# Hi and lo halves of normed inputs side by side: one 512-column matmul in place of two 256-column ones

## Chip, cores and metric

The kernel runs on one core of one Trainium2 chip. The metric is the device time of one execution in microseconds (us), less is better. The time before is 1701.62 us, the median of three runs (1701.26 to 1703.69).

## The reference, cut to what matters

One sequence of 256 tokens, 1024 wide, goes through a first block (a mixer, a cross-attention on a memory, a mixture of 32 experts) and then through two layers of a second block. All arithmetic is in float32. The change touches products of a normed input with a weight matrix: the queries of the cross-attention, and in each layer of the second block the hyena and the query/key projections and the first product of the feed-forward part.

```python
x = x + memory_cross_attention(rms_norm(x, g_xattn), rms_norm(mem, g_mem), w_q_x, w_kv_x, w_o_x)
...
for i in range(2):                                   # second block
    h = _rms_norm(x, norm_mix_pre[i])
    proj = h @ w_in[i]
    u_hy, q, k, v, g_out, gate_lr, u_pool, gate_logits = _split(proj, IN_SPLITS)
    y_hy = _hyena_mixer(u_hy, ...)                   # starts with a convolution over 3 tokens
    y_gla = _gla_mixer(q, k, v, g_out, gate_lr, ...) # q is scaled by 128 ** -0.5
    ...
    h = _rms_norm(x, norm_ffn_pre[i])
    a, b = _split(h @ ffn_w_up[i], (2816, 2816))
    a = _dwconv3_centred(a, ffn_conv_w[i], ffn_conv_b[i])
    y = (jax.nn.gelu(a, approximate=False) * b) @ ffn_w_down[i]
    x = x + _rms_norm(y, norm_ffn_post[i])
```

## The kernel before, in words

TensorE takes operands in a shortened float32 format (F32R). To keep float32 accuracy each operand is kept as two parts, hi (the rounded value) and lo (what the rounding left), and a product is made of three matmuls: hi times hi, hi times lo and lo times hi. `mm3` (lines 329 to 338) issues the three. Where the weights are the stationary operand they stand at lines 336 (weights' hi, input's hi), 337 (weights' hi, input's lo) and 338 (weights' lo, input's hi); where the input is stationary they stand at 332 to 334.

`norm` (line 430) makes a normed input: two tiles `hh` and `hl` of 128 partitions x 8 x 256 (feature within a group of 128, group, token), filled by transposes. `dense_t` (line 367) multiplies such an input with a "chunk" of weights, 1024 x 128 numbers held as 128 x 1024, and leaves the result transposed (128 output features x 256 tokens). A call handles two chunks, both into one bank of PSUM (the accumulators `acc`, four banks of 128 x 512), each in 8 steps over the features, so 8 x 3 matmuls of 256 columns for a chunk. These steps are called k-steps here. Then `consume(ps)` takes the bank off:
- for `w_q_x` (line 740) and `w_qk0`, `w_qk1` (line 1489) with one ScalarE copy of 128 x 512;
- for `w_hy0`, `w_hy1` (`hconv`, line 1496) with `conv3` (line 1328) twice, which reads PSUM with one ScalarE and two VectorE instructions (lines 1331, 1332, 1333);
- for `w_up0`, `w_up1` (`glu`, line 1648) with `conv3` on the one half, a Gelu on ScalarE (1651), a multiply by the other half on VectorE (1652) and a split of the result into hi and lo (455 on ScalarE, 456 on VectorE).

The weights come from HBM as plain float32 (`raw`) through the SP queue and are split on the chip, for each chunk: ScalarE writes `whi` (line 455, 128 x 1024), VectorE `wlo` (line 456). There are 5 buffers for `whi` (`NH`), 4 for `wlo` (`NL`). A split waits until the buffer is free, that is until TensorE has read the chunk that was in it.

The inputs that come out of `norm` with the pool `self.norms` are those of `w_q_x` (8 chunks), `w_qk` (8 chunks a layer), `w_hy` (12 chunks a layer) and `w_up` (40 chunks a layer): 128 chunks, 1024 k-steps, 3072 matmuls. Other inputs (`g_mix`, `g_mem`) use the same function with another pool. The same inputs also enter `dense_n`, where they are stationary and the weights stream in 512 columns (gates, values, pool).

The order of instructions on each engine is fixed when the program is built: a planner lists them by readiness and program order. On the chip each engine takes its own queue in that order, so an instruction that waits holds up what is queued behind it on its engine.

Of the kernel before, what the change touches and what calls it, by code (L numbers as in the profile page):

```python
# [22 lines left out]
F32 = mybir.dt.float32  # L23
F32R = mybir.dt.float32r
I32 = mybir.dt.int32
BF16 = mybir.dt.bfloat16
AF = mybir.ActivationFunctionType
OP = mybir.AluOpType
# [3 lines left out]
P = 128  # L32
D = 1024
S = 256
# [216 lines left out]
class Kernel:  # L251
# [114 lines left out]

    def dense_t(self, xT, name, chunks, consume):

        hi, lo = xT
        ps = self.acc().rearrange("p (j s) -> p j s", s=S)  # L370
        for j, chunk in enumerate(chunks):
            wh, wl = self.weights(name, chunk)
            for k in range(8):
                c = slice(k * P, k * P + P)
                self.mm3(ps[:, j], hi[:, k], lo[:, k], wh[:, c], wl[:, c], False, k == 0, k == 7)
        consume(ps)

# [50 lines left out]
    def norm(self, gname, pool, tag, g=None):  # L430

        nc = self.nc
        hi = pool.tile([P, 8, S], F32R, name=tag + "h", tag=tag + "h")
        lo = pool.tile([P, 8, S], F32R, name=tag + "l", tag=tag + "l")
        g = g or self.bcast(gname)

        def fill(t, xt, xg=None, r=None):
            if xg is None:
                xg, r = scaled(xt)
            nc.vector.tensor_scalar(xg[:, :512], xg[:, :512], r, None, op0=OP.mult)  # L440
            nc.scalar.activation(xg[:, 512:], xg[:, 512:], AF.Copy, scale=r)
            self.to_T(xg, hi, lo, t)

        def scaled(xt):
            ss = self.squares((xt[:, :512], xt[:, 512:]))
            xg = self.junk.tile([P, D], F32, name="xn", bufs=2)
            self.gained(xt, g, xg, 0)
            r = self.inv_norm(ss)
            self.gained(xt, g, xg, 1)
            return xg, r  # L450
        return (hi, lo), fill

    def split(self, hi, lo, src):

# [43 lines left out]
    def block1(self, outer, moe):  # L498
        nc, tc = self.nc, self.tc
        mm = nc.tensor.matmul  # L500
        x = self.x
        with ExitStack() as ctx:
            mix = ctx.enter_context(ExitStack())
            a = mix.enter_context(tc.tile_pool(name="mix", bufs=1, reuse_waits="tile"))

            nc.sync.dma_start(x[:, 0], self.ins["x"][0])
            hT, fill = self.norm("g_mix", outer, "hT")
# [63 lines left out]
            for t in range(2):  # L571
                ps = self.tp()
# [164 lines left out]
            self.load()  # L737
            qT = outer.tile([P, 8, S], F32, name="qk")
            for c in range(4):
                self.dense_t(qT_in, "w_q_x", (2 * c, 2 * c + 1), lambda ps, c=c: nc.scalar.activation(qT[:, 2 * c:2 * c + 2], ps, AF.Copy))  # L740
                if c < EARLY - 1:
                    self.load()
            sx = 1.0 / 16.0
# [38 lines left out]
            nc.sync.dma_start(wr, self.ins["w_r"])  # L782
            wr = wr.rearrange("p (k n) -> p k n", n=36)
            br = self.bcast("b_r", 0, 36, a, "br")
            hh, hl = (self.norms.tile([P, 2, D], F32R, name="h" + n, tag="h" + n) for n in "hl")
            L, W = (self.const.tile([P, 2, n], F32, name=k) for k, n in (("L", 36), ("W", NE)))
            A = self.const.tile([P, 2, NE], BF16, name="A")

# [569 lines left out]
    def mix(self, l, hT):  # L1358
# [3 lines left out]
        with ExitStack() as ctx:  # L1362
# [79 lines left out]
            nc.vector.tensor_sub(wlr[:, :, 96:], raw[:, :, 96:], wlr[:, :, 96:].bitcast(F32))  # L1442
            ps = self.acc()[:, :S]
            for k in range(8):
                for h in hT:
                    mm(ps, wlr[:, k], h[:, k], start=k == 0 and h is hT[0], stop=k == 7 and h is hT[1])
            lr = a.tile([P, S], F32R, name="lr")
            nc.scalar.activation(lr, ps, AF.Copy)
# [37 lines left out]

            qk = a.tile([P, 8, S], F32, name="qk", tag="qk")
            for c in range(4):
                self.dense_t(hT, f"w_qk{l}", (2 * c, 2 * c + 1), lambda ps, c=c: nc.scalar.activation(
                    qk[:, 2 * c:2 * c + 2], ps, AF.Copy, scale=P ** -0.5 if c < 2 else 1.0))  # L1490

            hw, hb = load(f"hy_conv_w{l}", [12, 3]), load(f"hy_conv_b{l}", [12])
            xv = a.tile([P, 8, S], F32, name="xv")
# [1 line left out]

            def hconv(n):
                def f(ps):
                    for j in range(2):
                        m = n + j
                        self.conv3(xv[:, m - 4] if m >= 4 else x0[:, m], ps[:, j], hw[:, m], hb[:, m:m + 1])  # L1500
                return f
            for n in (4, 8, 6, 10):
                self.dense_t(hT, f"w_hy{l}", (n, n + 1), hconv(n))
# [132 lines left out]
    def ffn(self, l, hT):  # L1636
        nc, tc = self.nc, self.tc
        x = self.x
        with ExitStack() as ctx:
            a = ctx.enter_context(tc.tile_pool(name=f"ffn{l}", bufs=1, reuse_waits="tile"))  # L1640
            cw = a.tile([P, NF, 3], F32, name="cw")
            nc.sync.dma_start(cw.rearrange("p a b -> p (a b)"), self.ins[f"ffn_conv_w{l}"])
            cb = a.tile([P, NF], F32, name="cb")
            nc.sync.dma_start(cb, self.ins[f"ffn_conv_b{l}"])
            hi, lo = (a.tile([P, NF, S], F32R, name="act" + n) for n in "hl")
            LEAD = 8

            def glu(j, ps):
                y = a.tile([P, S], F32, name="y", bufs=3)
                self.conv3(y, ps[:, 0], cw[:, j], cb[:, j:j + 1])  # L1650
                nc.scalar.activation(y, y, AF.Gelu)
                nc.vector.tensor_mul(y, ps[:, 1], y)
                self.split(hi[:, j], lo[:, j], y)
            for j in range(2):
                ps = self.tp()
                for n in range(4):
                    i, t = divmod(n, 2)
                    nc.tensor.transpose(ps[:, n * P:(n + 1) * P], self.up[:, t, (2 * j + i) * P:(2 * j + i + 1) * P], self.ident)
                glu(j, ps.rearrange("p (i s) -> p i s", i=2))
            for j in range(2, NF):  # L1660
                self.dense_t(hT, f"w_up{l}", (2 * j - 4, 2 * j - 3), partial(glu, j))
            g = self.bcast(f"norm_ffn_post{l}")
            ps = [[self.acc() for n in range(2)] for t in range(2)]
            if l == 0:
                hT, fill = self.norm("norm_mix_pre1", self.norms, "h")
            last = NF - LEAD
            ws = {}
            order = [(k, t, n) for k in range(last) for t in range(2) for n in range(2)]
            for k, t, n in order + ([(k, t, n) for t in range(2) for k in range(last, NF) for n in range(2)] if l == 0 else [(k, t, n) for t in range(2) for n in range(2) for k in range(last, NF)]):
                if k not in ws:  # L1670
                    ws[k] = self.weights(f"w_down{l}", k, k in range(last, NF - 4) and self.room(a, (f"held{k}",)))
                wh, wl = ws[k]
                tok, c = slice(t * P, (t + 1) * P), slice(n * 512, (n + 1) * 512)
                self.mm3(ps[t][n], hi[:, k, tok], lo[:, k, tok], wh[:, c], wl[:, c], True, k == 0, k == NF - 1)
                if k == NF - 1:
                    with tc.high_priority(100):
                        if n == 0:
                            take, end = self.post(g, t)
                        take(n, ps[t][n])
                        if n:  # L1680
                            end(None if l == 0 else lambda n, xn: nc.sync.dma_start(self.out[t][:, n * 512:(n + 1) * 512], xn))
                            if l == 0:
                                fill(t, x[:, t])
            return hT
# [21 lines left out]
```

## Time and profile before

| | us |
|---|---|
| median of three runs | 1701.62 |
| the profiled execution, timed | 1706.44 |
| its span in the profile | 1704.6 |
| TensorE matmul busy (share of the span) | 1635.3 (96%) |
| TensorE weight load busy | 1380.2 (81%) |
| VectorE busy | 1288.6 (76%) |
| ScalarE busy | 1133.9 (67%) |

PE is TensorE, PEld its weight loads, DVE VectorE, ACT ScalarE. A matmul's record runs from its start to the end of its result, and the records of neighbours overlap: its duration is not what it costs in a stream, which is the distance from its start to the start of the next. The mixture of experts lies between about 260 and 800 us; the second block from about 810 us to the end. In it the products with a transposed result lie at 878 to 935 us (`w_qk0`, `w_hy0`), 1078 to 1192 (`w_up0`), 1321 to 1378 (`w_qk1`, `w_hy1`) and 1522 to 1637 (`w_up1`); those of `w_q_x` at 170 to 194.

### The profile page before, as it was taken

The numbers are of one execution on the slowest core, as the hardware profiler recorded it, in microseconds if no ns is written. First come the engines' busy times: TensorE is split into PE (matmuls) and PEld (weight loads), VectorE is DVE, ScalarE is ACT, GpSimd is POOL, SyncE is SP. The second block draws the span as 40 slices with busy tenths as digits, with TensorE's granted clock in tenths as the row PEclk, the third lists the DMA queues.
The fourth block names the chain that finished last, engine by engine and source line by source line (L and its number), as shares of the span: only waits on it lengthen the run. The fifth ranks groups of instructions, "written<-read, shape, count | busy, mean of one in ns | idle before, by whom it ended". The sixth has DMA issues, their size and how long they took to land. (4 is left out here: it accounts for less than half of the span.)

```text
span 1704.6 us, 24749 instructions
## 1 busy us (share of the span) xinstructions
PE 1635.3 (96%) x9115; PEld 1380.2 (81%) x9115; DVE 1288.6 (76%) x1702; ACT 1133.9 (67%) x1576; POOL 30.3 (2%) x47
## 2 busy tenths in 40 slices
PE   7999987999999999988999999999999999999998
PEld 6897875777767777766799887999878998789986
DVE  7876566999989999998569667677556886667763
ACT  7765437899878899986667545555445864555552
POOL 1000000000000000000000000000000000000000
PEclk9999998999999999999999999999999999999999
DMA  8546537999999999994775356455756545635561
GB/s 292 199 155 204 191 148 266 352 380 373 381 380 380 402 386 408 416 400 170 253 252 186 128 189 223 143 185 182 238 171 222 202 150 181 214 130 185 183 198 62
DMA packets 94448, 415.92 MB, mean 244 GB/s; under 512 B 12324, under 2 KB 18868, under 8 KB 68468
## 3 DMA queue, kind: packets, MB, share of 16 engines
q1 hardware_dynamic: 89220, 405.91, 65.6%
q0 software_dynamic: 864, 6.29, 1.0%
q10 hardware_dynamic: 4240, 2.10, 0.4%
q8 instruction: 73, 1.20, 0.3%
q14 instruction: 51, 0.42, 0.1%
HBM read 411.12 MB, written 3.15 MB: 243 GB/s over the span
## 5 line engine op out<-in xcount | busy, mean ns | idle before, releaser
L456 DVE TENSOR_TENSOR wlo<-raw,whi 128x1024 fp32r<-128x1024 f32 x709 | 844.3, 1220 | 210.7 <-PE acc L333 80.7
L455 ACT ACTIVATE whi<-raw 128x1024 fp32r<-128x1024 f32 x711 | 728.7, 1055 | 230.6 <-PE acc L334 116.7
L337 PE MATMUL acc<-hl,whi 128*128 128x256 f32 x1024 | 289.9, 283 | 0.0
L338 PE MATMUL acc<-hh,wlo 128*128 128x256 f32 x1024 | 289.9, 283 | 0.0
L336 PE MATMUL acc<-hh,whi 128*128 128x256 f32 x1024 | 289.7, 283 | 0.0
L968 PE MATMUL misc<-whi,XT 128*128 128x512 f32 x512 | 227.5, 444 | 1.1 <-ACT XT L876 1.1
L969 PE MATMUL misc<-wlo,XT 128*128 128x512 f32 x512 | 208.5, 407 | 5.2 <-DVE wlo L456 5.1
L336 PEld LDWEIGHTS acc<-hh,whi 128*128 128x128 f32 x1024 | 196.5, 192 | 0.1
L337 PEld LDWEIGHTS acc<-hl,whi 128*128 128x128 f32 x1024 | 196.5, 192 | 0.0
L338 PEld LDWEIGHTS acc<-hh,wlo 128*128 128x128 f32 x1024 | 196.5, 192 | 0.0
L969 PEld LDWEIGHTS misc<-wlo,XT 128*128 128x128 f32 x512 | 97.9, 191 | 47.7 <-DVE wlo L456 22.4
L968 PEld LDWEIGHTS misc<-whi,XT 128*128 128x128 f32 x512 | 98.1, 192 | 30.4 <-issue 8.9
L332 PE MATMUL acc<-whi,hh 128*128 128x512 f32 x288 | 113.3, 395 | 0.6 <-ACT hh L423 0.5
L333 PE MATMUL acc<-wlo,hh 128*128 128x512 f32 x288 | 113.0, 393 | 0.1
L334 PE MATMUL acc<-whi,hl 128*128 128x512 f32 x288 | 112.4, 391 | 0.0
L985 PE MATMUL misc<-whi,at 128*128 128x512 f32 x256 | 105.8, 413 | 4.3 <-ACT whi L455 2.2
L986 PE MATMUL misc<-wlo,at 128*128 128x512 f32 x256 | 104.1, 407 | 1.7 <-DVE wlo L456 1.7
L944 PE MATMUL acc<-ye,DT 128*128 128x512 f32 x128 | 65.3, 595 | 0.0
L986 PEld LDWEIGHTS misc<-wlo,at 128*128 128x128 f32 x256 | 48.1, 188 | 20.7 <-DVE wlo L456 9.9
L332 PEld LDWEIGHTS acc<-whi,hh 128*128 128x128 f32 x288 | 54.3, 189 | 12.8 <-ACT hh L423 1.2
L334 PEld LDWEIGHTS acc<-whi,hl 128*128 128x128 f32 x288 | 54.2, 188 | 11.6 <-DVE hl L424 0.7
L333 PEld LDWEIGHTS acc<-wlo,hh 128*128 128x128 f32 x288 | 54.4, 189 | 11.3 <-DVE wlo L456 0.5
(466 smaller groups left out, 2724.0 us busy)
## 6 DMA issues: line engine op xcount, KB each, us to landing
raw<-in_w_egu SPq DMA_DIRECT2D x128, 1024.0 KB
raw<-in_w_ed SPq DMA_DIRECT2D x64, 1024.0 KB
raw<-in_w_up SPq DMA_DIRECT2D x80, 512.0 KB
raw<-in_w_gate SPq DMA_DIRECT2D x48, 512.0 KB
raw<-in_w_down SPq DMA_DIRECT2D x44, 512.0 KB
raw<-in_w_qk SPq DMA_DIRECT2D x24, 512.0 KB
raw<-in_w_out SPq DMA_DIRECT2D x24, 512.0 KB
raw<-in_w_br SPq DMA_DIRECT2D x24, 512.0 KB
```

The costliest lines, as they stand in the source:

```text
L332: mm(out, xh, wh, start=start, stop=False)
L333: mm(out, xh, wl, start=False, stop=False)
L334: mm(out, xl, wh, start=False, stop=stop)
L336: mm(out, wh, xh, start=start, stop=False)
L337: mm(out, wh, xl, start=False, stop=False)
L338: mm(out, wl, xh, start=False, stop=stop)
L455: self.nc.scalar.activation(hi, src, AF.Copy)
L456: self.nc.vector.tensor_sub(lo, src, hi.bitcast(F32))
L968: mm(p, l, wh[:, c], start=s == k == 0, stop=False)
L969: mm(p, l, wl[:, c], start=False, stop=s == 7 and k == 1)
L985: mm(p, l, wh[:, c], start=s == k == 0, stop=False)
L986: mm(p, l, wl[:, c], start=False, stop=s == 3 and k == 1)
```

## The change

The inputs from `self.norms` become one tile of 128 x 2 x 8 x 256 with hi and lo side by side. For them `dense_t` hands over to the new `dense_t2`: for each k-step one matmul of 512 columns multiplies the weights' hi part with the input's hi and lo together (256 columns each, into the two halves of a bank), and one of 256 columns multiplies the weights' lo part with the input's hi, into the first half. So a chunk now fills one bank, and a call takes two banks instead of one. The two halves are added when the bank is taken off, by the new `added`: ScalarE copies the second half to SBUF, VectorE adds the first half to it (with the scale, where there is one), for each chunk. `hconv` and `glu` then read the sum `u` in SBUF where they read PSUM before.

```diff
     def dense_t(self, xT, name, chunks, consume):
-        hi, lo = xT
+        hi, lo, *both = xT
+        if both:
+            return self.dense_t2(hi, both[0], name, chunks, consume)
...
+    def dense_t2(self, hi, both, name, chunks, consume):
+        mm = self.nc.tensor.matmul
+        ps = [self.acc().rearrange("p (i s) -> p i s", s=S) for _ in chunks]
+        for p, chunk in zip(ps, chunks):
+            wh, wl = self.weights(name, chunk)
+            for k in range(8):
+                c = slice(k * P, k * P + P)
+                mm(p, wh[:, c], both[:, :, k], start=k == 0, stop=False)
+                mm(p[:, 0], wl[:, c], hi[:, k], start=False, stop=k == 7)
+        consume(ps)
+
+    def added(self, to, ps, scale=1.0):
+        for j, p in enumerate(ps):
+            self.nc.scalar.activation(to[:, j], p[:, 1], AF.Copy, scale=scale)
+            if scale == 1.0:
+                self.nc.vector.tensor_add(to[:, j], p[:, 0], to[:, j])
+            else:
+                self.nc.vector.scalar_tensor_tensor(to[:, j], p[:, 0], scale, to[:, j], op0=OP.mult, op1=OP.add)
...
     def norm(self, gname, pool, tag, g=None):
-        hi = pool.tile([P, 8, S], F32R, name=tag + "h", tag=tag + "h")
-        lo = pool.tile([P, 8, S], F32R, name=tag + "l", tag=tag + "l")
+        if pool is self.norms:
+            both = pool.tile([P, 2, 8, S], F32R, name=tag, tag=tag)
+            parts = both[:, 0], both[:, 1], both
+        else:
+            parts = tuple(pool.tile([P, 8, S], F32R, name=tag + n, tag=tag + n) for n in "hl")
+        hi, lo = parts[:2]
...
-                self.dense_t(qT_in, "w_q_x", (2 * c, 2 * c + 1), lambda ps, c=c: nc.scalar.activation(qT[:, 2 * c:2 * c + 2], ps, AF.Copy))
+                self.dense_t(qT_in, "w_q_x", (2 * c, 2 * c + 1), partial(self.added, qT[:, 2 * c:2 * c + 2]))
...
-            hh, hl = (self.norms.tile([P, 2, D], F32R, name="h" + n, tag="h" + n) for n in "hl")
+            both = self.norms.tile([P, 2, 2, D], F32R, name="h", tag="h")
+            hh, hl = both[:, 0], both[:, 1]
...
-                self.dense_t(hT, f"w_qk{l}", (2 * c, 2 * c + 1), lambda ps, c=c: nc.scalar.activation(
-                    qk[:, 2 * c:2 * c + 2], ps, AF.Copy, scale=P ** -0.5 if c < 2 else 1.0))
+                self.dense_t(hT, f"w_qk{l}", (2 * c, 2 * c + 1), partial(
+                    self.added, qk[:, 2 * c:2 * c + 2], scale=P ** -0.5 if c < 2 else 1.0))
...
             def hconv(n):
                 def f(ps):
+                    u = a.tile([P, 2, S], F32, name="u")
+                    self.added(u, ps)
                     for j in range(2):
                         m = n + j
-                        self.conv3(xv[:, m - 4] if m >= 4 else x0[:, m], ps[:, j], hw[:, m], hb[:, m:m + 1])
+                        self.conv3(xv[:, m - 4] if m >= 4 else x0[:, m], u[:, j], hw[:, m], hb[:, m:m + 1])
...
+            def sum_glu(j, ps):
+                u = a.tile([P, 2, S], F32, name="u", bufs=2)
+                self.added(u, ps)
+                glu(j, u)
...
             for j in range(2, NF):
-                self.dense_t(hT, f"w_up{l}", (2 * j - 4, 2 * j - 3), partial(glu, j))
+                self.dense_t(hT, f"w_up{l}", (2 * j - 4, 2 * j - 3), partial(sum_glu, j))
```

## Rows read from the trace of the kernel before

**Rows 1.** The page's first part: busy time (share of the span) xinstructions, by engine.

```profile
PE 1635.3 (96%) x9115; PEld 1380.2 (81%) x9115; DVE 1288.6 (76%) x1702; ACT 1133.9 (67%) x1576; POOL 30.3 (2%) x47
```

**Rows 2.** Windows: length, busy (xcount) of PE, PEld, DVE, ACT, POOL; PEclk, DMA, GB/s.

```profile
1078.00:1192.00 114.00, 114.00 (x952) 114.00 (x952) 83.05 (x123) 67.16 (x103) 0.00 (x0) 1.00 0.54 176
...
878.00:935.00 57.00, 57.00 (x475) 56.82 (x475) 49.42 (x69) 44.78 (x65) 0.00 (x0) 1.00 0.62 211
...
170.50:193.50 23.00, 23.00 (x193) 23.00 (x192) 9.80 (x8) 10.43 (x12) 0.00 (x0) 1.00 0.56 182
```

**Rows 3.** Timeline of PE in `w_up0`: start us, duration us, engine, line, operation.

```profile
1100.01 0.28 PE L336 MATMUL acc<-hh,whi 128*128 128x256 f32 x1
...
1103.97 0.28 PE L336 MATMUL acc<-hh,whi 128*128 128x256 f32 x1
```

**Rows 4.** Timeline of PE in the gates' product of layer 0.

```profile
985.69 0.39 PE L332 MATMUL acc<-whi,hh 128*128 128x512 f32 x1
...
987.96 0.39 PE L333 MATMUL acc<-wlo,hh 128*128 128x512 f32 x1
```

**Rows 5.** Timeline of PE in `w_down0`.

```profile
1194.62 0.39 PE L332 MATMUL acc<-whi,acth 128*128 128x512 f32 x1
...
1195.78 0.39 PE L334 MATMUL acc<-whi,actl 128*128 128x512 f32 x1
```

**Rows 6.** Groups by form: ... xcount | busy us, mean ns | idle before, releasers.

```profile
L456 DVE TENSOR_TENSOR wlo<-raw,whi 128x1024 fp32r<-128x1024 f32 x709 | 844.3, 1220 | 210.7 <-PE acc L333 80.7 <-PE acc L338 53.9 <-ACT whi L455 46.7
L455 ACT ACTIVATE whi<-raw 128x1024 fp32r<-128x1024 f32 x711 | 728.7, 1055 | 230.6 <-PE acc L334 116.7 <-PE acc L337 51.7 <-PE misc L968 23.2
...
L336 PE MATMUL acc<-hh,whi 128*128 128x256 f32 x1024 | 289.7, 283 | 0.0
...
L336 PEld LDWEIGHTS acc<-hh,whi 128*128 128x128 f32 x1024 | 196.5, 192 | 0.1
L332 PE MATMUL acc<-whi,hh 128*128 128x512 f32 x288 | 113.3, 395 | 0.6 <-ACT hh L423 0.5
...
L1333 DVE SCALAR_TENSOR_TENSOR y<-acc,cw,y 128x255 f32<-128x255 f32 x40 | 19.3, 483 | 1.4
...
L1652 DVE TENSOR_TENSOR y<-acc,y 128x256 f32<-128x256 f32 x40 | 16.7, 418 | 1.1 <-ACT y L1651 1.1
...
L1319 ACT ACTIVATE fk<-tp 128x256 f32<-128x256 f32 x16 | 6.2, 385 | 8.4 <-PE tp L1316 8.4
```

**Rows 7.** Waits between 1090 and 1180 us (`w_up0`): us in total, times, longest.

```profile
DVE wlo L456 <- PE acc L338: 13.4, 31, 0.5
...
ACT whi L455 <- PE acc L337: 11.2, 15, 0.7
```

**Rows 8.** Timeline of DVE over one call of `w_up0`, waits in brackets.

```profile
1135.13 1.22 DVE L456 TENSOR_TENSOR wlo<-raw,whi 128x1024 fp32r<-128x1024 f32 x1 [0.41 <-PE acc L338]
1136.56 0.48 DVE L1332 SCALAR_TENSOR_TENSOR y<-acc,cw,y 128x255 f32<-128x255 f32 x1 [0.20 <-ACT y L1331]
1137.07 0.48 DVE L1333 SCALAR_TENSOR_TENSOR y<-acc,cw,y 128x255 f32<-128x255 f32 x1
1138.01 1.22 DVE L456 TENSOR_TENSOR wlo<-raw,whi 128x1024 fp32r<-128x1024 f32 x1 [0.45 <-PE acc L338]
1139.15 0.42 DVE L1652 TENSOR_TENSOR y<-acc,y 128x256 f32<-128x256 f32 x1
1140.05 0.43 DVE L456 TENSOR_TENSOR actl<-y,acth 128x256 fp32r<-128x256 f32 x1 [0.48 <-ACT acth L455]
1140.89 1.23 DVE L456 TENSOR_TENSOR wlo<-raw,whi 128x1024 fp32r<-128x1024 f32 x1 [0.41 <-PE acc L338]
```

**Rows 9.** Windows, as in group 2, of the end of `w_qk0` and `w_hy0`.

```profile
903.00:935.00 32.00, 32.00 (x269) 32.00 (x268) 30.92 (x46) 24.34 (x41) 0.00 (x0) 1.00 0.59 196
```

**Rows 10.** Timeline of DVE after `w_hy0`.

```profile
943.22 0.74 DVE L1536 COPY_PREDICATED Pm<-cst,misc 128x512 f32<-128x512 int32 x1 [3.72 <-PE misc L1534]
```

**Rows 11.** Windows of PE alone: length, PE busy (xcount), PEclk, DMA, GB/s.

```profile
1481.00:1484.40 3.40, 3.27 (x10) 0.50 0.66 194
```

More of the change, by code (lines that the diff above doesn't have):

```diff
@@ L450, in scaled @@
             return xg, r
-        return (hi, lo), fill
+        return parts, fill
     def split(self, hi, lo, src):
@@ L1444, in mix @@
             for k in range(8):
-                for h in hT:
+                for h in hT[:2]:
                     mm(ps, wlr[:, k], h[:, k], start=k == 0 and h is hT[0], stop=k == 7 and h is hT[1])
```

## The prediction

> **What bounds the kernel now.** I began with the page's busy times: TensorE's matmuls are at 96% of the span, the other engines at 76% or less [rows 1]. That share is no price, since records of matmuls overlap, so I went on to windows over the stages that the change touches. There PE has no gap in a whole stage, at the full granted clock (1.00, the 2.4 GHz level): 114.00 of 114.00 us with 952 matmuls in `w_up0`, 57.00 of 57.00 in `w_qk0` and `w_hy0`, 23.00 of 23.00 in `w_q_x` [rows 2]; the second layer repeats the first two. So these stages, some 368 us together (3072 matmuls x 0.12), end when PE is through with them. What one matmul costs there is read from the timeline, from start to start: 256 columns take 3.96 us / 33 = 0.120 us [rows 3], which 114.00 / 952 confirms [rows 2]. The group's means (283 ns for 256 columns, 395 for 512 [rows 6]) are latencies; by them a k-step would fall from 849 to 678 ns and the kernel by some 175 us, which rows 3 rule out. The weight loads (192 ns each [rows 6]) lie beside the matmuls in the same way, so 1024 fewer of them are worth nothing by themselves.
>
> VectorE comes second. In `w_up0` it waits for PE to free a `wlo` buffer, 13.4 us in 31 waits, and ScalarE for a `whi` buffer, 11.2 us in 15 [rows 7]: both keep ahead of PE. Late in `w_hy0` that is not so: VectorE is busy 30.92 of 32.00 us [rows 9], while PE still has no gap.
>
> **Part 1, the matmuls.** A k-step costs 3 x 0.120 = 0.360 us now. After the change it is one 512-column matmul and one of 256. 512 columns with the same `whi` and `hh` buffers, roles swapped, take 2.27 us / 10 = 0.227 [rows 4]; in `w_down0` 1.16 / 5 = 0.232 [rows 5]. Nothing in the trace shows a stream whose 512 columns come from two places 8 KB apart. The ends are therefore 0.227 and 0.240, the price of two 256-column matmuls; I take 0.230, between the two rows that the trace has. The second matmul stays at 0.120. So 0.350 us, a saving of 10 ns (ends 13 and 0) for each of 1024 k-steps: 9.6 us in the second block (960 of them), of which 6.4 in the two `w_up` stages (640) and 3.2 in the two mixing stages (320), and 0.6 in `w_q_x`.
>
> Two 256-column matmuls cost 240 ns and one of 512 costs 227 to 232 [rows 3 to 5], and on this difference the whole gain rests. The Trainium skill (TensorE: Matmul & The Clock Gate, "Wait — 56ns, not 53.3ns?") speaks against so much: a warm matmul follows the last one after N / 2.4 GHz plus about 2.5 ns, so merging two saves one 2.5 ns, 2.6 us in all. The trace does not agree with that price: 120 and 227 ns stand 13 and 14 ns above N / 2.4 GHz.
>
> **Part 2, ScalarE and VectorE in `w_up`.** For each call two copies from PSUM (385 ns, the nearest row) and two adds (418 ns, the row of a product of a PSUM half and an SBUF tile) come in [rows 6]; `conv3` and the multiply read SBUF instead, taken at no change. A call lasts 5.76 us now and 16 x 0.350 = 5.60 after. VectorE's 5.76 us are 0.41 + 0.45 of waiting for PE, 0.20 + 0.48 for ScalarE, and 4.22 of work and issue [rows 8]. With the adds the work is 5.06; with the same waits for ScalarE 5.74. The first chunk's bank is done half a call (2.8 us) before the second's, so its add can stand in the 0.48 us wait: 5.74 - 0.42 = 5.32, plus 0.20 (rows 8's wait for a ScalarE result) for the other add behind its copy, 5.52. That is below 5.60 by 0.08 us: PE stays the bound, narrowly. ScalarE is busy 67.16 / 114.00 x 5.76 = 3.4 us a call [rows 2], 4.2 with the copies, and its wait for PE (11.2 / 15 = 0.75 [rows 7]) is about as long as the two copies. So I cost this part at nothing; the cover is those waits for PE, and without it the price is in the second rival. Behind a late add on VectorE stand the next `wlo` splits, for which PE waits; behind a late copy on ScalarE stand the `whi` splits. No gain below nothing is possible here, since PE has no gap to give back [rows 2].
>
> **Part 3, the same in the mixing stages.** Each layer gets 8 additions in `w_qk` (4 scaled at 483 ns, 4 at 418: 3.6 us) and 12 in `w_hy` (5.0 us) [rows 6], 8.6 us of VectorE. The first 3.6 fall mostly before 903 us, where VectorE is busy 49.42 - 30.92 = 18.5 of 25 us [rows 2, 9], and cost nothing. The 5.0 fall where 1.1 us is free [rows 9]; 3.9 remain, and the `wlo` splits queue behind them. Four `wlo` buffers hold chunks of 24 x 0.120 = 2.9 us, so part of it is paid by eating into that lead, and VectorE can catch up right after the stage, where it waits 3.72 us for PE [rows 10]. Bounds: 0 and 8.6 us a layer. I take 2, what is left of 3.9 if the lead gives two thirds of a chunk; 4 us for both layers.
>
> **Part 4, the rest.** In `w_q_x` VectorE (9.80) and ScalarE (10.43 of 23.00 us [rows 2]) have room, so its 0.6 us are gained there; whether a later stage takes them back the rows don't show: 0 to 0.6, I take 0.3. PSUM: a call takes two of four banks, so a bank must be read within one call's length where three stood before; the adds read it earlier than `conv3` and the multiply did, so nothing. `hh` and `hl` in one tile are released together; both are read last by neighbouring matmuls, so nothing. No DMA is added or moved; the DMA share is 0.54 to 0.62 in these stages [rows 2], and a stage shorter by 3% stays below its limit.
>
> **Sum.** -9.6 - 0.3 + 4.0 = -5.9 us. The profiled execution took 1706.44 us (its span is 1704.6, with 1.8 around it), so 1700.5 for one like it; it lies 4.8 above the median of the runs shown, and against that median the forecast is 1701.62 - 5.9 = 1695.7 us.
>
> **Rivals.** (1) The merged matmul costs what the two did, 0.240 a pair: part 1 is nil, and with PE no faster the mixing stages lose perhaps 1 us each: 1703.6, no change. For it: no row has the split stream. Against it: rows 4 and 5. By the skill's 2.5 ns the time would be 1701.62 - 2.6 + 2 = 1701.0, also no change.
> (2) Slower: VectorE becomes the bound in `w_up`. If the planner leaves both adds behind their copies and fills none of the waits, its call is 5.74 + 0.20 = 5.94 us, PE waits for `wlo`, and the 40 calls lose 0.18 each against 5.76: +7.2, with -3.2 + 4.0 - 0.3 elsewhere 1709.3 us. It decides from a VectorE call of 5.76 us on. For it: the margin of 0.08 us, and the chain of copy, add, `conv3`, Gelu, multiply, split that goes to and fro between two engines. Against it: first-chunk banks are ready early, and the planner can set splits into the waits.
> (3) The best: 0.227 for the pair and no stall anywhere: 13 ns x 1024 = 13.3 us, 1688.3 us.
> (4) Noise of a new order elsewhere: a stretch at half the granted clock (0.50, the 1.2 GHz level, 3.40 us long with ten matmuls [rows 11]) can come or go, 1.7 us each.
>
> **How the numbers follow.** Chances: forecast 0.52 (its own range 1691 to 1700), rival 1 0.13, rival 2 0.18, rival 3 0.12, something else 0.05. The range runs from rival 3 to rival 2, 1687 to 1709. A measurement of this kernel can tell about 0.2%, 3.4 us, from no change: faster means below 1698.2, slower above 1705.0. Faster takes 0.45 of the forecast, rival 3 and 0.02 of the rest: 0.59. Same: 0.07 of the forecast, 0.10 of rival 1 and 0.02: 0.19. Slower: rival 2, 0.03 of rival 1 and 0.01: 0.22.
>
> **What would show it.** In the timeline of the changed kernel the 512-column matmul should be followed after 0.227 to 0.232 us and the 256-column one after 0.120; a call of `w_up` should last 5.60 us with PE gapless and VectorE still waiting a little for PE at `wlo`. If PE waits for `wlo` there, rival 2 holds; if the pair is at 0.360 a k-step, rival 1. In `w_hy` I expect PE to wait about 2 us a layer, for `wlo` or for a bank. Wrong would be the forecast, too, if the mixing stages lost the full 8.6 us.

## The result, and the profile after

The changed kernel takes 1713.11 us (median of 6 runs, 1711.69 to 1716.63), the kernel before on the same chip 1701.44: a ratio of 1.0066, 95% interval 1.0055 to 1.0077. It is slower by 11.7 us, where 5.9 us less was forecast, and it lies above the whole range of 1687 to 1709. Its profiled execution took 1716.63 us, with a span of 1714.9, 10.2 longer than that of before.

The page's busy times first, engine by engine, to be read against [rows 1]:

```profile
PE 1634.5 (95%) x8091; PEld 1327.3 (77%) x8091; DVE 1322.2 (77%) x1830; ACT 1167.5 (68%) x1692; POOL 30.3 (2%) x47
```

They show 1024 matmuls fewer and 128 VectorE instructions more than before, and nothing of the loss. That comes out by stage. The table has, for the two profiled executions, the time from the start of a stage's first matmul to the start of its last one, or between two such points.

| stretch | before, us | after, us | difference |
|---|---|---|---|
| up to the first matmul of `w_qk0` | 876.2 | 873.6 | -2.7 |
| `w_qk0` and `w_hy0` | 58.8 | 65.4 | +6.6 |
| from there to the last matmul of `w_up0` | 257.3 | 257.8 | +0.4 |
| from there to the first of `w_qk1` | 126.5 | 128.3 | +1.8 |
| `w_qk1` and `w_hy1` | 58.8 | 65.0 | +6.2 |
| from there to the last of `w_up1` | 259.2 | 257.1 | -2.1 |

The end behind `w_up1` is the same in both (67.8 us). The differences are taken before rounding. So the two mixing stages lose 12.8 us and the rest gains 2.5. Where they lose it is in the list of waits of PE between 873 and 940 us of the changed kernel (us in total, times, longest):

```profile
PE acc L389 <- DVE qk L398: 3.1, 1, 3.1
PE acc L390 <- DVE wlo L484: 2.1, 1, 2.1
```

In the kernel before PE had no gap there [rows 2]. The timeline of PE shows both waits in `w_qk0`, at its last chunks (start, duration, line, tiles, the wait in brackets), and what comes behind them:

```profile
894.61 0.62 PE L389 MATMUL acc<-h,whi 128*128 128x512 f32 x2
898.35 0.50 PE L389 MATMUL acc<-h,whi 128*128 128x512 f32 x1 [3.12 <-DVE qk L398]
900.91 0.58 PE L390 MATMUL acc<-h,wlo 128*128 128x256 f32 x1 [2.06 <-DVE wlo L484]
901.29 0.63 PE L389 MATMUL acc<-h,whi 128*128 128x512 f32 x1
901.72 0.41 PE L390 MATMUL acc<-h,wlo 128*128 128x256 f32 x1
901.93 0.63 PE L389 MATMUL acc<-h,whi 128*128 128x512 f32 x1
```

PE starts a chunk's bank only when the add at line 398 has read the bank's former chunk; then it needs a `wlo` that is not there yet. From 901.29 on a k-step takes 0.64 us. The windows over this stretch and its twin in layer 1 (us, PE busy, granted clock, DMA share, GB/s) say why:

```profile
901.30:906.60 5.30, 5.30 (x18) 0.50 0.78 239
1352.80:1358.10 5.30, 5.30 (x21) 0.57 0.74 230
```

PE came out of two waits, and the granted clock stood at 0.50, the 1.2 GHz level. The matmuls in the 5.34 us from 901.29 to 906.63 take 2.9 us at the full clock: 2.4 lost. From start to start the waits cost a little more than their own length: from 894.61 to 898.35 there are two matmuls of 0.236 us, 3.27 too long, from 898.35 to 900.91 one, 2.32 too long, and the next start comes 0.26 late (0.38 instead of 0.12). So 3.27 + 2.32 + 0.26 + 2.4 = 8.2 us are lost in layer 0; the cheaper matmuls give 1.6 back (below), and 6.6 is what the table shows. Layer 1 has the same two waits, 3.12 and 2.05 us, and a shorter stretch at 0.50 (4.68 us, 2.1 lost): 7.9 us in all.

Why VectorE was late stands in its own queue. Its timeline in the changed kernel:

```profile
883.56 1.23 DVE L484 TENSOR_TENSOR wlo<-raw,whi 128x1024 fp32r<-128x1024 f32 x1 [1.33 <-issue]
885.90 0.42 DVE L400 SCALAR_TENSOR_TENSOR qk<-acc,qk 128x256 f32<-128x256 f32 x1 [1.12 <-ACT qk L396]
889.13 2.29 DVE L1493 TENSOR_TENSOR b<-b,en 128x2048 f32<-128x2048 f32 x1 [2.81 <-ACT en L1492]
891.34 0.42 DVE L400 SCALAR_TENSOR_TENSOR qk<-acc,qk 128x256 f32<-128x256 f32 x1
891.68 1.22 DVE L1494 TENSOR_SCALAR b<-b 128x2048 f32<-128x2048 f32 x1
892.81 0.42 DVE L398 TENSOR_TENSOR qk<-acc,qk 128x256 f32<-128x256 f32 x1
893.14 2.43 DVE L1497 TENSOR_TENSOR_SCAN b<-cst,b 128x256 f32<-128x256 f32 x4
895.49 2.41 DVE L1499 TENSOR_TENSOR_SCAN b<-cst,b 128x256 f32<-128x256 f32 x4
897.82 0.15 DVE L1503 COPY ends<-b 128x16 f32<-128x16 f32 x1
897.88 0.42 DVE L398 TENSOR_TENSOR qk<-acc,qk 128x256 f32<-128x256 f32 x1
898.22 0.16 DVE L1504 COPY ends<-b 128x16 f32<-128x16 f32 x1
898.30 1.42 DVE L1510 TENSOR_TENSOR b<-b,ends 128x256 f32<-128x256 f32 x4
899.64 1.22 DVE L484 TENSOR_TENSOR wlo<-raw,whi 128x1024 fp32r<-128x1024 f32 x1
```

And the same place in the kernel before:

```profile
886.48 1.23 DVE L456 TENSOR_TENSOR wlo<-raw,whi 128x1024 fp32r<-128x1024 f32 x1 [1.71 <-PE acc L338]
889.58 1.23 DVE L456 TENSOR_TENSOR wlo<-raw,whi 128x1024 fp32r<-128x1024 f32 x1 [1.88 <-ACT whi L455]
892.81 2.29 DVE L1464 TENSOR_TENSOR b<-b,en 128x2048 f32<-128x2048 f32 x1 [2.00 <-ACT en L1463]
895.02 1.22 DVE L456 TENSOR_TENSOR wlo<-raw,whi 128x1024 fp32r<-128x1024 f32 x1
896.15 1.22 DVE L1465 TENSOR_SCALAR b<-b 128x2048 f32<-128x2048 f32 x1
897.29 1.22 DVE L456 TENSOR_TENSOR wlo<-raw,whi 128x1024 fp32r<-128x1024 f32 x1
898.42 2.43 DVE L1468 TENSOR_TENSOR_SCAN b<-cst,b 128x256 f32<-128x256 f32 x4
```

The operations on `b` are the gate chain of the mixer's other branch, each waiting for the last, with eight scans in it (4.7 us in one piece). Before, two `wlo` splits stood in the chain's two places. In the changed kernel two adds stand there; the splits come behind the scans, and so does the next add, at 897.88. TensorE needs both. VectorE's order changed by more than these two places: ahead of the scans it does seven splits from 875.63 us on in the kernel before, and in the changed one four from 872.94 on, beside five adds; the scans start 22.2 us after the stage's first matmul before and 19.6 in the changed kernel. So the scans did not come late; the planner put them ahead of work that PE needs sooner.

### The profile page after: what moved, and what is told of

Same layout as the page of the kernel before. It is cut to its first block, busy times and chain, and to the rows that moved or that the text cites. A ratio compares the mean times of both kernels' runs of the same rounds, so it can differ in the third digit from the quotient of the medians.

```text
span 1714.9 us, 22924 instructions
## 1 busy us (share of the span) xinstructions
PE 1634.5 (95%) x8091; PEld 1327.3 (77%) x8091; DVE 1322.2 (77%) x1830; ACT 1167.5 (68%) x1692; POOL 30.3 (2%) x47
## 5 line engine op out<-in xcount | busy, mean ns | idle before, releaser
L389 PE MATMUL acc<-h,whi 128*128 128x512 f32 x1024 | 365.7, 401 | 6.2 <-DVE qk L398 6.2
L390 PE MATMUL acc<-h,wlo 128*128 128x256 f32 x1024 | 289.2, 283 | 4.1 <-DVE wlo L484 4.1
L389 PEld LDWEIGHTS acc<-h,whi 128*128 128x128 f32 x1024 | 194.6, 190 | 54.0 <-DVE qk L398 7.1
L390 PEld LDWEIGHTS acc<-h,wlo 128*128 128x128 f32 x1024 | 195.9, 191 | 5.1 <-DVE wlo L484 4.7
L332 PE MATMUL acc<-whi,h 128*128 128x512 f32 x288 | 114.3, 398 | 0.6 <-ACT h L447 0.5
L333 PE MATMUL acc<-wlo,h 128*128 128x512 f32 x288 | 113.9, 396 | 0.1
L334 PE MATMUL acc<-whi,h 128*128 128x512 f32 x288 | 113.3, 394 | 0.0
L332 PEld LDWEIGHTS acc<-whi,h 128*128 128x128 f32 x288 | 55.0, 191 | 13.1 <-ACT h L447 1.2
L334 PEld LDWEIGHTS acc<-whi,h 128*128 128x128 f32 x288 | 54.8, 190 | 12.1 <-DVE h L448 0.9
L333 PEld LDWEIGHTS acc<-wlo,h 128*128 128x128 f32 x288 | 54.7, 190 | 11.5 <-DVE wlo L484 0.5
L1014 PEld LDWEIGHTS misc<-whi,at 128*128 128x128 f32 x256 | 48.1, 188 | 16.0 <-ACT whi L483 4.5
L334 PE MATMUL acc<-whi,actl 128*128 128x512 f32 x144 | 56.8, 395 | 0.0
```

Of the source, the lines that this page charges most:

```text
L332: mm(out, xh, wh, start=start, stop=False)
L333: mm(out, xh, wl, start=False, stop=False)
L334: mm(out, xl, wh, start=False, stop=stop)
L389: mm(p, wh[:, c], both[:, :, k], start=k == 0, stop=False)
L390: mm(p[:, 0], wl[:, c], hi[:, k], start=False, stop=k == 7)
L1014: mm(p, l, wh[:, c], start=s == k == 0, stop=False)
```

## The experiments

Theory A was that reading: `w_qk`'s adds, and the `wlo` splits that lose their places with them, queue on VectorE behind the gate chain. Its rivals: B, the adds cost where they are put, `w_up` and `w_hy` included; C, two banks a call are too few whatever reads them. Each ratio is to the kernel before on the same chip, five rounds. An edit is against the changed kernel where nothing else is said.

**The change without `w_qk`** (there as before):

```diff
-                self.dense_t(hT, f"w_qk{l}", (2 * c, 2 * c + 1), partial(
-                    self.added, qk[:, 2 * c:2 * c + 2], scale=P ** -0.5 if c < 2 else 1.0))
+                self.dense_t(hT[:2], f"w_qk{l}", (2 * c, 2 * c + 1), lambda ps, c=c: nc.scalar.activation(
+                    qk[:, 2 * c:2 * c + 2], ps, AF.Copy, scale=P ** -0.5 if c < 2 else 1.0))
```

> The changed kernel, but w_qk in both layers is made as before: three 256-column matmuls a k-step into one bank, taken off by one ScalarE copy of 128x512. Theory A (in the changed kernel VectorE has the additions of w_qk and the wlo splits queued behind the long gate operations of the GLA branch, TensorE waits there 3.3 us for a bank and 2.3 us for wlo in each layer, and then runs at the 1.2 GHz level for a while, some 8.4 us a layer in all): about 2 x 8.4 us less than the changed kernel's 1713.1, with 2 x 64 k-steps x 7 ns = 0.9 us given back: 1697 us, below the kernel before, and no gap of TensorE over 1 us between 873 and 940 us. Theory B (the additions cost time wherever they stand, since VectorE is full in w_hy and nearly so in w_up): 1705 us or more.

1701.46 us (1696.74 to 1705.06), 0.9989 (0.9977 to 1.0001). PE has no gap in `w_qk`; a mixing stage takes 58.2 us. The gap went as theory A said, and the loss with it; a gain over the kernel before, which it expected too (1697 us), is not clear, since the interval reaches 1.

**`w_qk` alone**, against the kernel before: the call of `w_qk` is the changed one, those of `w_hy`, `w_up` and `w_q_x` stay.

> The kernel before with the change in w_qk alone (both layers); w_q_x, w_hy and w_up as before. Theory A: the whole loss comes with it, 1701.4 + 2 x 8.4 - 0.9 = 1717 us, with the same gaps of TensorE and the same stretch at the 1.2 GHz level. Theory B: at most a third of the added VectorE work lies here (16 of 120 additions), so under 1705 us.

1717.99 us (1716.15 to 1720.16), 1.0086 (1.0073 to 1.0099), with both waits, 3.1 and 1.9 us, in layer 0. 8 of a layer's 60 chunks thus carry more than the whole loss.

**`w_up` alone**, in the same way:

> The kernel before with the change in w_up alone (640 of the 1024 k-steps). Theory A: TensorE is the bound there in the changed kernel as well (no gap in 114.00 us) and a k-step costs 0.353 instead of 0.360 us: 640 x 7 ns = 4.5 us less than before, about 1697 us. Theory B (additions cost here too): no gain, 1701 us or more.

1697.09 us (1692.29 to 1698.43), 0.9967 (0.9954 to 0.9980). The adds of `w_up` cost nothing that one could see, and this version beats both kernels.

**The matmuls without the adds**: the banks' second halves (weights' hi times input's lo) are written and never read, which leaves that term out of the result.

```diff
-            self.nc.scalar.activation(to[:, j], p[:, 1], AF.Copy, scale=scale)
-            if scale == 1.0:
-                self.nc.vector.tensor_add(to[:, j], p[:, 0], to[:, j])
-            else:
-                self.nc.vector.scalar_tensor_tensor(to[:, j], p[:, 0], scale, to[:, j], op0=OP.mult, op1=OP.add)
+            self.nc.scalar.activation(to[:, j], p[:, 0], AF.Copy, scale=scale)
...
-                        self.conv3(xv[:, m - 4] if m >= 4 else x0[:, m], u[:, j], hw[:, m], hb[:, m:m + 1])
+                        self.conv3(xv[:, m - 4] if m >= 4 else x0[:, m], ps[j][:, 0], hw[:, m], hb[:, m:m + 1])
```

> All matmuls as in the changed kernel, two banks a call, but the additions are left out: the second half of each bank (weights' hi times input's lo) is dropped, and the first half is used as the sum. conv3 and the multiply read PSUM as before; w_qk and w_q_x have one ScalarE copy of 128x256 a chunk. This shows what TensorE saves with no VectorE work added. Theory A: 1024 x 7 ns = 7 us less than before and no waits for a bank: 1694 us. Theory C (two banks a call are too few, whoever empties them): gaps of TensorE for a bank in w_qk remain, over 1702 us.

1695.89 us (1694.46 to 1699.47), 0.9964 (0.9950 to 0.9977), PE without a wait in the mixing stage of layer 0, two banks a call or not (in layer 1 one of 0.4 us, for `wlo`). C falls, and B with `w_up` alone. A stands, but it has two halves: the add that holds a bank (D) and the late `wlo` split (E). The next two runs take them apart.

**ScalarE frees the bank**, VectorE adds later from SBUF. The copies `w` take the space (`tag`) in which `xv`, the result of `w_hy`'s convolution, lies later:

```diff
+            w = a.tile([P, 4, 2, S], F32, name="w", tag="xv")
+
+            def late(c, ps):
+                for j, p in enumerate(ps):
+                    n = 2 * c + j
+                    nc.scalar.activation(w[:, n % 4], p, AF.Copy, scale=P ** -0.5 if c < 2 else 1.0)
+                    nc.vector.tensor_add(qk[:, n], w[:, n % 4, 0], w[:, n % 4, 1])
...
-                self.dense_t(hT, f"w_qk{l}", (2 * c, 2 * c + 1), partial(
-                    self.added, qk[:, 2 * c:2 * c + 2], scale=P ** -0.5 if c < 2 else 1.0))
+                self.dense_t(hT, f"w_qk{l}", (2 * c, 2 * c + 1), partial(late, c))
```

> As the changed kernel, but in w_qk the banks are taken off whole by ScalarE (one copy of 128x512 a chunk) and VectorE adds the two halves from SBUF. So TensorE no longer waits for VectorE to get a bank back; the wlo splits of the last w_qk chunks still stand behind the scans in VectorE's queue. Theory D (the bank held by a late add is the cause): the gaps in w_qk go, some 8 us a layer come back, about 1697 us. Theory E (the wlo splits that the adds pushed behind the scans are the cause, or are enough by themselves): the wait for a bank goes, but TensorE comes to its wait for wlo earlier and waits there for about 5 us and then runs at the half clock: about 1713 us, as the changed kernel.

1713.53 us (1710.76 to 1717.24), 1.0068 (1.0053 to 1.0084): no better, as E has it. Its waits of PE from 873 to 945:

```profile
PE acc L390 <- DVE wlo L484: 4.6, 1, 4.6
PE acc L389 <- ACT w L1522: 1.2, 1, 1.2
```

**The splits go first**, on ScalarE and VectorE, by their precedence in the planner; the adds have none:

```diff
-            wh, wl = self.weights(name, chunk)
+            with self.tc.high_priority(300 if name.startswith(("w_qk", "w_hy")) else 0):
+                wh, wl = self.weights(name, chunk)
```

> As the changed kernel, but the weight splits of the mixing stage's chunks have precedence in VectorE's and ScalarE's order, so that the wlo splits of the last w_qk chunks stand ahead of the scans; the adds that free the banks come behind the scans. Theory D (the bank held by a late add): TensorE waits for the bank, now for longer than 3 us, in w_qk, and the time is 1713 us or more. Theory E (late wlo splits): with these splits early w_qk has no gap to speak of, about 1697 us.

1709.39 us (1706.32 to 1711.71), 1.0048 (1.0035 to 1.0061), between what D and E expected. The wait changes its name:

```profile
PE acc L390 <- DVE qk L401: 3.8, 1, 3.8
PE acc L390 <- DVE qk L399: 0.7, 1, 0.7
```

The shorter of the two waits is for an add behind the scans, as expected. The longer one is for an add ahead of them, which VectorE's queue holds up behind the chain's first operations and a split:

```profile
896.67 1.22 DVE L485 TENSOR_TENSOR wlo<-raw,whi 128x1024 fp32r<-128x1024 f32 x1
897.81 1.22 DVE L1495 TENSOR_SCALAR b<-b 128x2048 f32<-128x2048 f32 x1
898.95 0.42 DVE L401 SCALAR_TENSOR_TENSOR qk<-acc,qk 128x256 f32<-128x256 f32 x1
899.28 2.43 DVE L1498 TENSOR_TENSOR_SCAN b<-cst,b 128x256 f32<-128x256 f32 x4
```

Either half alone keeps PE waiting for 4.5 to 5.8 us in layer 0; to take one away uncovers the other.

**Both mends at once**:

> As the changed kernel, with both mends of the last two runs at once: in w_qk ScalarE takes each bank off whole (128x512) and VectorE adds from SBUF, and the mixing stage's wlo splits stand ahead of the scans in VectorE's order. By the theory that has come out of the runs (two operations of VectorE on TensorE's path, the add that frees a bank and the wlo split, were pushed behind the gate chain and the scans, and either alone stalls TensorE for about 4 to 5 us with a half clock behind it) w_qk now has no gap over 1 us, a mixing stage lasts about 57 to 58 us instead of 65, and the time is about 1697 us. If instead VectorE simply has too little time in w_qk for 8 more operations (a rival: then no order helps), a gap of some us stays and the time is 1705 or more.

1709.94 us (1707.34 to 1713.13), 1.0045 (1.0028 to 1.0061). This was not expected by the theory. `w_qk` is mended (one wait of 0.4 us, for ScalarE), and the loss turns up later, in `w_hy`:

```profile
PE acc L390 <- DVE u L399: 4.1, 2, 2.4
PE acc L390 <- ACT w L1523: 0.4, 1, 0.4
```

Five of the eight adds of `w_qk` now come behind the scans, at 905.93, 908.82 and 910.63 us, ahead of the first adds of `w_hy`, and these free the banks. So the rival was half right: order heals `w_qk`, but VectorE seems to have no time to spare after it. Two buffers may have a part in this: `w_hy`'s `conv3` can write `xv` only when the last add of `w_qk` has read `w`, and the next copy to `u`, which has one buffer, starts at 919.51, when `conv3` has read the last one (918.84, 0.48 long); the wait of 2.4 us ends behind the add of that copy, at 920.37.

**Both mends, `w_hy` as before** (its `conv3` reads PSUM again) puts that to the test:

```diff
-                    u = a.tile([P, 2, S], F32, name="u")
-                    self.added(u, ps)
...
-                self.dense_t(hT, f"w_hy{l}", (n, n + 1), hconv(n))
+                self.dense_t(hT[:2], f"w_hy{l}", (n, n + 1), hconv(n))
```

> As the run with both mends of w_qk, but w_hy as in the kernel before (three 256-column matmuls, conv3 reads PSUM, no adds), its wlo splits with the same precedence: VectorE has 12 operations, about 5 us, less to do in each mixing stage after the scans. In the run with both mends VectorE was busy 34.13 of the 35 us from 900 on and TensorE waited in w_hy for its adds. If VectorE's time after the gate chain is what lacks (the w_qk adds that come after the scans push the rest back), TensorE has no gap over 1 us in w_hy here, a mixing stage lasts 58 to 59 us and the time is about 1699 us (1709.9 less twice 5.5). If the late adds of w_qk delay w_hy whatever VectorE's load, a wait of 2 to 4 us stays in w_hy and the time is 1705 or more.

1701.20 us (1697.98 to 1704.00), 0.9983 (0.9972 to 0.9994), 2 us above what was expected and with the expected shape: a mixing stage takes 58.9 us and PE is gapless in `w_hy`. The windows from 900 to 935 us (PE, PEld, VectorE, ScalarE), first with both sets of adds, then with those of `w_hy` gone:

```profile
900.00:935.00 35.00, 30.88 (x179) 26.74 (x178) 34.13 (x60) 27.27 (x49) 0.00 (x0) 1.00 0.49 159
```

```profile
900.00:935.00 35.00, 35.00 (x295) 35.00 (x294) 34.72 (x58) 27.23 (x45) 0.00 (x0) 1.00 0.51 174
```

VectorE is as full in both, so its busy share does not tell them apart; PE's gaps do. The stage bears the adds of `w_hy` (the first run) or, with both mends, those of `w_qk`; in none of the orders tried did it bear both. Whether VectorE's time was short or the buffers of `w` and `u` delayed the adds was not separated, since this run has no `u`; `u` alone does not cost, for the run with `w_qk` as before has it and no gap in `w_hy`.

**GpSimd adds** in place of VectorE, from the copies that ScalarE makes, as in the run where ScalarE frees the bank:

```diff
+                    nc.gpsimd.tensor_add(qk[:, n], w[:, n % 4, 0], w[:, n % 4, 1])
```

> As the changed kernel, but in w_qk ScalarE copies the bank whole and GpSimd adds the two halves from SBUF, so that VectorE's queue holds no add of w_qk and its wlo splits stand in the gaps of the gate chain as in the kernel before. Theories D and E both: neither the bank nor the splits are late, no gap in w_qk, about 1696 us (between the 1701.46 of the run with w_qk as before, less 320 x 10 ns of w_qk's matmuls in two layers' 128 k-steps, i.e. 1.3 us, and the 1695.89 of the run without adds). Theory B (an add costs wherever it is): 1705 or more.

1708.20 us (1706.96 to 1710.82), 1.0040 (1.0027 to 1.0053): a miss. VectorE's timeline has no add of `w_qk`, and yet it is slower:

```profile
890.74 1.77 DVE L484 TENSOR_TENSOR wlo<-raw,whi 128x1024 fp32r<-128x1024 f32 x1
892.43 1.77 DVE L1494 TENSOR_SCALAR b<-b 128x2048 f32<-128x2048 f32 x1
894.11 1.76 DVE L484 TENSOR_TENSOR wlo<-raw,whi 128x1024 fp32r<-128x1024 f32 x1
895.79 2.97 DVE L1497 TENSOR_TENSOR_SCAN b<-cst,b 128x256 f32<-128x256 f32 x4
```

The split at 1.22 us takes 1.77 while GpSimd adds, four scans 2.97 instead of 2.43. PE waits 3.1 us for `wlo` again. ScalarE, with its copies of 0.58 us, also comes later to the `whi` split that the `wlo` split needs (888.88 us). Which of the two weighs more was not separated.

**The old matmuls with the new banks and adds**: from the second k-step on the merged matmul is two again.

```diff
-                mm(p, wh[:, c], both[:, :, k], start=k == 0, stop=False)
+                if k == 0:
+                    mm(p, wh[:, c], both[:, :, k], start=True, stop=False)
+                else:
+                    mm(p[:, 0], wh[:, c], hi[:, k], start=False, stop=False)
+                    mm(p[:, 1], wh[:, c], both[:, 1, k], start=False, stop=False)
```

> As the changed kernel with its banks and its adds everywhere, but for the second to the eighth k-step the 512-column matmul is two of 256 columns again, so that TensorE pays the old price (about 0.360 us a k-step). What the merged matmul saves is then the difference to the changed kernel: 896 k-steps by 7 to 13 ns, 6 to 12 us: about 1721 us. If the saving were gone because the adds hide it in w_up: 1713.

1716.81 us (1716.43 to 1717.91), 1.0088 (1.0075 to 1.0102). Against the changed kernel's 1.0066 that is 0.0022, 3.7 us, less than expected, though the two intervals allow anything up to 8. The trace is sharper: a `w_up` stage lasts 115.8 us here and 113.8 in the changed kernel, 2.0 for 40 of 128 chunks, so 6.3 for all. The merged matmul does save time, at the lower end of what was expected.

**`w_up` and `w_q_x`**, the rest as before, the search for a better version:

> The kernel before with the change in w_up and in w_q_x only; w_qk and w_hy as before. No gap in the mixing stages; w_up 111.7 or 113.8 us a layer instead of 115. If w_q_x keeps its 0.4 us: about 1696.7 us, against 1697.1 for w_up alone; at any rate faster than both the kernel before and the changed one. If the adds in w_q_x hold up the attention behind it: 1699 or more.

1699.42 us (1693.56 to 1702.84), 0.9978 (0.9964 to 0.9992). `w_q_x` keeps its 0.4 us in the trace (22.49 us instead of 22.91), but the time can't tell this version from that with `w_up` alone, 0.9967; both are faster than the kernel before. Of the 6.1 us between their two traces, 4.2 are in `w_up` itself: both stages took 113.8 us here and 111.7 there, with the same code (the last section has these two paces).

## Why the prediction was wrong, point by point

**The bound.** Right: in `w_up` of the changed kernel PE is still without a gap, and the stage ends when it is through. Windows of 1083 to 1197 us, to be read against [rows 2]:

```profile
1083.00:1197.00 114.00, 114.00 (x649) 98.88 (x648) 92.61 (x162) 79.75 (x144) 0.00 (x0) 1.00 0.55 176
```

**Part 1, the matmuls.** The mechanism held, and the size came out at two values. In `w_up` a k-step takes 353.3 ns in both layers of the changed kernel, 346.7 in both of the version with `w_up` alone, against 360.0 before: 6.7 or 13.3 ns where 10 was taken, with ends 0 and 13. PE's timeline from 1099.67 us in the changed kernel, 0.24 us for 512 columns and 0.12 for 256:

```profile
1099.67 0.40 PE L389 MATMUL acc<-h,whi 128*128 128x512 f32 x1
1099.91 0.28 PE L390 MATMUL acc<-h,wlo 128*128 128x256 f32 x1
1100.03 0.40 PE L389 MATMUL acc<-h,whi 128*128 128x512 f32 x1
```

In the profiled execution `w_up` and `w_q_x` gained 704 x 6.7 ns = 4.7 us. The mixing stages ran at 353 ns up to the waits (58 k-steps) and at 347 behind the stretch at half clock (93): 58 x 6.7 + 93 x 13.3 ns = 1.6 us a layer. That is 8.0 in all, where 9.6 and 0.3 were counted. The 2.5 ns that the Trainium skill gives (TensorE: Matmul & The Clock Gate, "Wait — 56ns, not 53.3ns?") would be too little in either case.

**Part 2, `w_up`.** Right. VectorE is busy 92.61 of 114 us (83.05 before [rows 2]), and it still waits 0.4 to 0.6 us for PE at its `wlo` splits. Rival 2 gave 1709.3 us, near the result, by a mechanism that did not occur.

**Part 3, the mixing stages.** This is the step that failed, in its sentence on `w_qk`: the first 3.6 us of adds "fall mostly before 903 us ... and cost nothing", because VectorE is busy 18.5 of 25 us there. The window was too coarse. Cut at 892 us, the kernel before reads:

```profile
876.00:892.00 16.00, 16.00 (x133) 15.75 (x132) 9.68 (x14) 13.83 (x18) 0.54 (x1) 1.00 0.85 293
892.00:903.00 11.00, 11.00 (x94) 11.00 (x93) 10.19 (x12) 7.94 (x10) 0.00 (x0) 1.00 0.43 150
```

Of the 7.1 us idle in these two windows, 6.3 lie before 892. The changed kernel's stage starts 2.7 us earlier, so 892 is its 889.3, and by then it has done three of its eight adds (878.85, 881.82, 885.90; the fourth comes at 891.34), since their banks fill one by one and ScalarE's copies stand behind the gates' operations. So the idle time was over before the work was there. What was missing beside it is the queue: an add behind the chain waits for eight scans, whatever the share of busy time. The term was taken as 2 us a layer and measured 8.2 and 7.9, near the bound of 8.6 but by another way, in `w_qk` and not in `w_hy`; 8.6 is the adds' own busy time, which does not bound such a wait, so its nearness is chance. The 2 us themselves, argued for `w_hy`, did not come as a stall: in the run without `w_qk`'s change the stage lost nothing (58.2 us, 0.6 less than before), and PE waited 1.4 us a layer after its end, for ScalarE's `Pm`.

**Part 4.** `w_q_x` gained 0.4 us, within its 0 to 0.6. The sentence on PSUM failed: "the adds read it earlier ... so nothing" went by the order of the program, and in VectorE's queue one add stood behind the scans, so that PE waited 3.1 us for a bank.

**The sum.** Matmuls, `w_q_x` among them, -8.0, the mixing stages 8.2 + 7.9 = +16.1: +8.1 of the 10.2 us between the two spans. The remaining 2.1 lie in the stretches between and were not traced to a cause. The clock's part, 2.4 + 2.1 us, is in no term of the prediction; it knew the 0.50 level [rows 11], but only as something that comes and goes, not as the price of a wait. What was said to make the forecast wrong did: the mixing stages lost nearly the full 8.6 us, before what the matmuls gave back.

## What to carry to other kernels

Do not price added operations by the idle share of a window: put each into its engine's queue, ask when its input is there, what stands ahead of it in one piece, and who waits for it; idle time that is over before the input exists is worth nothing. A release (of a PSUM bank, of a buffer) given from a busy engine to another busy engine, behind a long dependent chain, stalls the bound engine, and here the granted clock put 2.4 and 2.1 us on top of 5.9 us of waiting a layer. A change that helps a stream can be kept where its extra work has cover, here in `w_up`, and left out where it has none: that version took 1697.09 us, 0.3% less than the kernel before.

## What the hardware showed that was not expected

One stream had two paces. The alternation of 512 and 256 columns ran at 353.3 ns a k-step for whole stages of some runs and at 346.7 for whole stages of others, the two layers of one execution among them. PE's timeline of `w_up0` with the change in `w_up` alone, at 0.23 and 0.12 us:

```profile
1099.70 0.39 PE L389 MATMUL acc<-h,whi 128*128 128x512 f32 x1
1099.93 0.28 PE L390 MATMUL acc<-h,wlo 128*128 128x256 f32 x1
1100.05 0.39 PE L389 MATMUL acc<-h,whi 128*128 128x512 f32 x1
```

In both layers of the changed kernel the pace was the slower one ahead of the waits in `w_qk` and the faster one behind them, so it can change at a stall; what sets it stays open. It is worth 2.1 us a `w_up` stage (113.8 or 111.7).

The half clock came with the waits. Over 873 to 945 us and 1315 to 1395 us the granted clock averaged 1.00 in both layers of the kernel before and of the five versions whose waits there stayed at 1.4 us or less. It averaged 0.95 to 0.98 in both layers of the changed kernel and of the five versions whose longest wait there was 2.9 us or more. With both mends (two waits in each layer's `w_hy`, the longer 2.4 us) it was 1.00 in layer 0 and 0.98 in layer 1.

VectorE and GpSimd slow each other. Where both worked, VectorE's split took 1.77 us instead of 1.22, and two adds on GpSimd 4.05 us instead of 0.74 each. The Trainium skill (GPSIMD Engine Reference, "1. Specifications") says that GpSimd's access to SBUF is shared with VectorE and contends with VectorE's instructions that read two SBUF inputs or run in a two-port mode; the split, which reads `raw` and `whi`, agrees with it.
